# Where the moving operands of the dense products lie in SBUF: right end instead of beside the weights, xs tiles 2112 bytes apart

## The chip, the cores and the metric

One NeuronCore of one Trainium2 chip runs the whole program in one launch. The metric is device time in microseconds. The kernel before was timed in three runs.

## What is computed

The reference is a two-layer encoder trunk on 256 tokens of width 2048, with 256 memory tokens, all in float32. Cut to what matters here:

```python
for i in range(2):
    h = rmsnorm(x, norm_w[i])
    kv = rmsnorm(mem, mem_norm_w[i]) @ w_kv_mem[i]           # 2048 x 4096
    if i == 0:   # h @ w_in (14336 columns), windowed means, group product, cross-attention, SiLU gate
        y = pooling_branch(h, ...)
    else:        # h @ w_in (16512 columns), gated delta rule in chunks of 64, cross-attention, gate
        y = deltanet_branch(h, ...)
    x = x + y @ w_out[i]                                     # 6144 x 2048
return rmsnorm(x, final_norm_w)
```

Nearly all arithmetic is in products of some 256 rows of activations with large weight matrices that are read once.

## The kernel before, in words

Activations stand transposed: features on the 128 partitions, the 256 tokens along the row. A dense product forms 128 output features at a time. A weight block of 128x128 is the stationary operand, a tile of 128x256 is the moving one, and the sum over the input features builds up in one PSUM tile `pd`.

To keep float32 precision at the speed of the one-pass float32r format, each factor is split into a high and a low part. Weights arrive by DMA in units of 128 x 1024 floats (512 KB) into `wr` (`fetch`, L204, four buffers). ScalarE casts a unit into `wh` (L218), and VectorE forms `wl` = `wr` - `wh` (L220), three buffers each (`stage`, L211). A unit holds eight blocks of 128x128, each 512 bytes of a partition's row. An activation tile has shape [128, 2, 256]: its first 1024 bytes are the high part, the next 1024 the low part. Each 128x128 block then takes three matmuls, for instance in `dense` (L237):

```python
mm(ps, wh[:, kk, :], xh, k == 0, False)
mm(ps, wh[:, kk, :], xl, False, False)
mm(ps, wl[:, kk, :], xh, False, k == n - 1)
```

There are three kinds of these activation tiles. `xs` (16 buffers, written in `split_x`, L307) is the normalized input of a layer, the moving operand of the input product. The same buffers hold the raw memory tokens in `mem_tiles`, and in the last group the gated output (`new_y`, L414, with `last`). `y` (12 buffers) is the gated output, the moving operand of `out_piece` (L417). `ms` (16 buffers) holds the normalized memory tokens and later the pooled groups: the moving operand of the product for the keys in `mem_kv` (L373) and of the group product in `mix_jobs` (L607), and the stationary operand of the product for the values, in which `wh` and `wl` move with 512 columns. Other temporaries of the first part (softmax, decay gates) take turns in the `ms` buffers.

Buffers come from pools. `keep` and `work` last for the whole kernel, and `work` holds `wr`, `wh`, `wl`, `xs`, `y` and small tiles. `mp` holds `ms` and the attention's keys and values, and is given up before the second part, the delta rule, whose pool `gp` then takes its place.

TensorE's order is set by hand: `Flow` (L83) interleaves the dense jobs with the dependent chains (softmax, decay, matrix inversion, delta rule) by a small model of time. Line 184 is the matmul in the helper `mm`, so all matmuls but transposes have that line, and the tiles tell them apart.

Of the kernel before, what the change touches and what calls it, by code (L numbers as in the profile page):

```python
# [24 lines left out]
XA_SCALE = 512 ** -0.5  # L25
DN_SCALE = 128 ** -0.5

# buffers per tag, and dense steps between two looks at the chains
W_RAW_BUFS = 4
W_SPLIT_BUFS = 3  # L30
PS_DENSE = 3
# [1 line left out]
CHAIN_BUFS = 6  # L33
SQ_BUFS = 3
SLICE = 2
# priorities of the weight staging and of the parts of a chain on ScalarE and VectorE
P_STAGE = 600
P_UA = 600
P_INV = 600
P_NORM = 600  # L40
# how long the tensor engine leaves a step of a chain to the other engines, in units of US ns
US = 1300.0
Y_CONV = 9.0
Y_INV = 14.2
# [36 lines left out]


class Flow:  # L83
    """Interleaves dense weight products with the dependent chains, in the order the tensor engine issues them."""

    def __init__(self):
        self.now, self.tasks, self.jobs, self.active = 0.0, [], [], None
# [50 lines left out]
def trunk_kernel(  # L138
# [21 lines left out]

    keep = ctx.enter_context(tc.tile_pool(name="keep", bufs=1))
    work = ctx.enter_context(tc.tile_pool(name="work", bufs=2))
    psd = ctx.enter_context(tc.tile_pool(name="psd", bufs=PS_DENSE, space=PSUM))
    psa = ctx.enter_context(tc.tile_pool(name="psa", bufs=PS_CHAIN, space=PSUM))
    psk = ctx.enter_context(tc.tile_pool(name="psk", bufs=2, space=PSUM))

    def wt(shape, dt, tag, bufs):
        return work.tile(shape, dt, tag=tag, name=tag, bufs=bufs)

    def pa(n):  # L170
        t = psa.tile([P, 512], F32, tag="a", name="pa")
# [135 lines left out]
    def split_x(layer, row):  # L307
        for k in range(KT):
            xn = wt([P, S], F32, "xn", SQ_BUFS)
            V.scalar_tensor_tensor(  # L310
                out=xn, in0=xT[:, k, :], scalar=small[:, SM_NW + layer * KT + k : SM_NW + layer * KT + k + 1],
                in1=row, op0=ALU.mult, op1=ALU.mult,
            )
            xs[k] = wt([P, 2, S], F32R, "xs", KT)
            split_to(xs[k], xn)
            yield 0.7

# [3 lines left out]
    def mem_tiles(layer):  # L321
        if layer == 0:
            tiles = []
            for c in range(8):
                fetch(c + 1 if c < W_RAW_BUFS else W_RAW_BUFS)
                mt = wt([P, 2, S], F32, "xs", KT)
                nc.sync.dma_start(out=mt, in_=mem_d[:, 2 * c : 2 * c + 2, :])
                tiles.append(mt)
            for c in range(8):
                if c < W_SPLIT_BUFS:  # L330
                    stage(c + 1)
                mem_split(layer, 2 * c, tiles[c])
            return tiles
        for c in range(8):
            mt = wt([P, 2, S], F32, "xs", KT)
            nc.gpsimd.dma_start(out=mt, in_=mem_d[:, 2 * c : 2 * c + 2, :])
            mem_split(layer, 2 * c, mt)
            yield 0.8
# [3 lines left out]
    def mem_split(layer, k0, mt):  # L342
        for i in range(2):
            k = k0 + i
            w = small[:, SM_MW + layer * KT + k : SM_MW + layer * KT + k + 1]
            t = mp.tile([P, 2, S], F32R, tag="ms", name="ms", bufs=KT)
            A.activation(out=t[:, 0, :], in_=mt[:, i, :], func=AF.Copy, scale=w)  # L347
            V.scalar_tensor_tensor(  # L348
                out=t[:, 1, :], in0=mt[:, i, :], scalar=w, in1=t[:, 0, :].bitcast(F32),
                op0=ALU.mult, op1=ALU.subtract,  # L350
            )
            ms[k] = t
# [59 lines left out]
        return g  # L412

    def new_y(last=False):  # L414
        return wt([P, 2, S], F32R, "xs", KT) if last else wt([P, 2, S], F32R, "y", 12)

    def out_piece(src, ys, nk, *flags, acc=None, done=None):  # L417
        per = HC // nk
# [38 lines left out]
    def softmax_chain(layer, h, q, pT, done):  # L457
        yield 0.6
        kT = kv["k", layer]
        sc = pa(512).rearrange("p (s m) -> p s m", s=2)  # L460
        for st in range(2):
            for kk in range(4):
                mm(sc[:, st, :], q[kk][:, st * P : (st + 1) * P], kT[:, 4 * h + kk, :], kk == 0, kk == 3)
        mx = wt([P, 2], F32, "mx", 2)
        V.tensor_reduce(out=mx, in_=sc, axis=AX.X, op=ALU.max)
        nb = wt([P, 2], F32, "nb", 2)
        V.tensor_scalar(out=nb, in0=mx, scalar1=-XA_SCALE, scalar2=None, op0=ALU.mult)
        p = mp.tile([P, 2, S], F32, tag="ms", name="xp", bufs=KT)
        sm = wt([P, 2], F32, "smx", 2)
        for st in range(2):  # L470
            A.activation(
                out=p[:, st, :], in_=sc[:, st, :], func=AF.Exp, bias=nb[:, st : st + 1], scale=XA_SCALE,
                accum_out=sm[:, st : st + 1],
            )
        rs = wt([P, 2], F32, "rs", 2)
        V.reciprocal(out=rs, in_=sm)
        V.tensor_scalar(out=rs, in0=rs, scalar1=0.5, scalar2=None, op0=ALU.mult)
        for st in range(2):
            V.tensor_scalar(
                out=p[:, st, :], in0=p[:, st, :], scalar1=rs[:, st : st + 1], scalar2=None, op0=ALU.mult  # L480
            )
        yield 5.0
        pt = pa(512).rearrange("p (m s) -> p m s", m=2)
        for mt in range(2):
            for st in range(2):
                transpose(pt[:, mt, st * P : (st + 1) * P], p[:, st, mt * P : (mt + 1) * P], ident)
        t = mp.tile([P, 2, S], F32, tag="ms", name="xpt", bufs=KT)
        for mt in range(2):
            A.activation(out=t[:, mt, :], in_=pt[:, mt, :], func=AF.Copy, scale=rmem["col"][:, mt : mt + 1])
        pT[h] = t  # L490
        done.set(flow.now + 1500)

    def attention(layer, wsrc, ct_q, ct_g, xready, kvready):
# [5 lines left out]
        def q_jobs(h):  # L499
            q = [None] * 4  # L500

            def mk(kk):
                def post(ps):
                    if kk % 2 == 0:
                        q2 = mp.tile([P, 2, S], F32, tag="ms", name="xq", bufs=KT)
                        q[kk], q[kk + 1] = q2[:, 0, :], q2[:, 1, :]
                    A.copy(out=q[kk], in_=ps)
                    if kk == 3:
                        flow.spawn(softmax_chain(layer, h, q, pT, soft[h]))

                return post

            for kk in range(4):
                dense([wsrc[ct_q + 4 * h + kk, i] for i in range(2)], get_xs, mk(kk), xready, kvready)
# [19 lines left out]

    mp_cm = tc.tile_pool(name="mp", bufs=1)
    mp = mp_cm.__enter__()
    mem_ready, mem_done, x_ready, kv_ready = Flag(), Flag(), Flag(), Flag()

    def start_up():
# [33 lines left out]
    def u_jobs(g):  # L573
        for c in range(8):
            def post(ps, c=c):
                if c == 0:
                    cnts[g] = mp.tile([P, S], F32, tag="ms", name="cnt", bufs=KT)
                    nc.gpsimd.dma_start(out=cnts[g], in_=cnt_d[:, g, :])
                    if g == 0:
                        V.tensor_scalar(  # L580
                            out=scale_h, in0=small[:, SM_PS : SM_PS + 32], scalar1=0.5, scalar2=None, op0=ALU.mult
                        )
                u = ub[c % 2]
                A.copy(out=u[:, 8 : S + 8], in_=ps)
                src, n = u, S + 16
                for lv in range(g + 1):
                    step = 1 << lv
                    n -= step
                    dst = mp.tile([P, S + 16], F32, tag="ms", name="pacc", bufs=KT)
                    V.tensor_tensor(out=dst[:, 0:n], in0=src[:, 0:n], in1=src[:, step : step + n], op=ALU.add)  # L590
                    src = dst
                off = 8 - WINDOWS[g] // 2
                m = wt([P, S], F32, "xn", SQ_BUFS)
                V.tensor_tensor(out=m, in0=src[:, off : off + S], in1=cnts[g], op=ALU.mult)
                V.tensor_tensor(out=m, in0=m, in1=u[:, 8 : S + 8], op=ALU.subtract)
                t = mp.tile([P, 2, S], F32R, tag="ms", name="ms", bufs=KT)
                split_to(t, m)
                pooled[g][c] = t
                if c == 7:
                    pflag[g].set(flow.now + 5000)  # L600
# [91 lines left out]
        flow.spawn(decay_chain(ps))  # L692

    def decay_chain(ps):
        mask = mp.tile([P, 2, P], F32, tag="ms", name="mask", bufs=KT)
        nc.gpsimd.dma_start(out=mask, in_=cst_d[:, CS_MASK:CS_W].rearrange("p (d m) -> p d m", d=2))
        V.tensor_copy(out=identr, in_=ident)
        V.tensor_copy(out=selr, in_=cst[:, CS_SEL : CS_SEL + 64])
# [7 lines left out]
        V.tensor_scalar(out=nwh, in0=small[:, SM_DN : SM_DN + 1], scalar1=0.5, scalar2=None, op0=ALU.mult)  # L706

        def mt(shape, name):
            return mp.tile(shape, F32, tag="ms", name=name, bufs=KT)

        cum = [[mt([P, 384], "cum") for _ in range(2)] for _ in range(2)]
        for d in range(2):
# [58 lines left out]
    g_jobs(3)  # L771
    n_first = len(flow.jobs)

    # second part: the jobs of the delta-rule groups
    kqs = [[None] * 4 for _ in range(8)]
    kq_state = [None] * 8
    kq_done = [Flag() for _ in range(8)]
# [445 lines left out]
    engines = ENGINES  # L1223
    with tc.manual_schedule(engines=engines):
        flow.run(len(flow.jobs) - n_first)
    mp_cm.__exit__(None, None, None)
    gp = ctx.enter_context(tc.tile_pool(name="gp", bufs=1))
    gpool.append(gp)
# [159 lines left out]
```

## Time and profile before

| | |
|---|---|
| median of three runs | 2592.03 us |
| lowest and highest run | 2589.52 and 2594.63 us |
| span of the profiled execution | 2590.5 us |
| mean granted clock of TensorE | 0.998 |
| instructions in the profile | 53005 |

The profile is one execution with a span of 2590.5 us from the first to the last instruction. No time of its own is listed for that execution beside the span; the span lies between the lowest and the highest of the three runs, and 1.5 us below their median. A matmul's duration in the profile reaches from its start to the modelled end of its pipeline, so durations of successive matmuls overlap, and the busy share says little on the rate; the distance from one start to the next gives the rate.

### The profile page before, as it was taken

The numbers are of one execution on the slowest core, as the hardware profiler recorded it, in microseconds if no ns is written. First come the engines' busy times: TensorE is split into PE (matmuls) and PEld (weight loads), VectorE is DVE, ScalarE is ACT, GpSimd is POOL, SyncE is SP. The second block draws the span as 40 slices with busy tenths as digits, with TensorE's granted clock in tenths as the row PEclk, the third lists the DMA queues.
The fourth block names the chain that finished last, engine by engine and source line by source line (L and its number), as shares of the span: only waits on it lengthen the run. The fifth ranks groups of instructions, "written<-read, shape, count | busy, mean of one in ns | idle before, by whom it ended". The sixth has DMA issues, their size and how long they took to land.

```text
span 2590.5 us, 53005 instructions
## 1 busy us (share of the span) xinstructions
PE 2566.3 (99%) x21996; PEld 2510.7 (97%) x21996; DVE 1788.2 (69%) x3317; ACT 1238.0 (48%) x1946; POOL 15.5 (1%) x44
## 2 busy tenths in 40 slices
PE   8999999999999999999999999999999999999998
PEld 7899999999999999998999999999999999999998
DVE  6564455656557576674546557989889797979786
ACT  5444434434444443554344445555545555565544
POOL 0000000000000000000000000000000000000000
PEclk9999999999999999999999999999999999999999
DMA  7654455555555555655554545535344454535353
GB/s 241 219 185 160 159 172 166 184 185 187 184 185 187 184 185 187 204 190 189 190 186 156 164 161 167 167 116 164 127 155 136 138 163 133 164 127 166 125 175 103
DMA packets 120817, 436.17 MB, mean 168 GB/s; under 512 B 13728, under 2 KB 13984, under 8 KB 120576
## 3 DMA queue, kind: packets, MB, share of 16 engines
q1 hardware_dynamic: 118080, 426.06, 50.4%
q0 software_dynamic: 1776, 5.64, 0.7%
q8 instruction: 172, 2.82, 0.4%
q10 hardware_dynamic: 720, 1.08, 0.1%
q14 instruction: 69, 0.57, 0.1%
HBM read 430.63 MB, written 2.10 MB: 167 GB/s over the span
## 4 chain that ended last, share of the span: by engine, by line
PE 96%; DVE 2%; ACT 1%; issue 0%; DMA 0%; POOL 0%; DVEq 0%
PE pd L184 86%; PE pa L184 9%; PE kk L184 1%; DVE wl L220 1%; PE pa L188 0%; ACT wh L218 0%; DMA xs<-in_mem_dram 0%; DVE ms L348 0%; DVE o L1264 0%; DMA wr<-in_wv_dram 0%; DVE Dg L983 0%; DVE cacc L795 0%; DVE L L985 0%; ACT ms L347 0%; DVE itmp L993 0%
## 5 line engine op out<-in xcount | busy, mean ns | idle before, releaser
L220 DVE TENSOR_TENSOR wl<-wr,wh 128x1024 fp32r<-128x1024 f32 x802 | 981.1, 1223 | 609.1 <-ACT wh L218 607.2
L184 PE MATMUL pd<-xs,wh 128*128 128x256 f32 x7328 | 1351.4, 286 | 2.8 <-DVE gt L411 2.1
L218 ACT CAST wh<-wr 128x1024 fp32r<-128x1024 f32 x802 | 841.0, 1049 | 1043.3 <-PE pd L184 839.8
L184 PEld LDWEIGHTS pd<-xs,wh 128*128 128x128 f32 x7328 | 1143.5, 192 | 7.4 <-DVE gt L411 2.3
L184 PE MATMUL pd<-xs,wl 128*128 128x256 f32 x3664 | 1036.5, 283 | 0.0
L184 PEld LDWEIGHTS pd<-xs,wl 128*128 128x128 f32 x3664 | 702.1, 192 | 0.0
L184 PE MATMUL pd<-y,wh 128*128 128x256 f32 x2944 | 524.0, 280 | 1.1 <-DVE y L258 1.1
L184 PEld LDWEIGHTS pd<-y,wh 128*128 128x128 f32 x2944 | 449.7, 187 | 1.8 <-DVE y L258 1.3
L184 PE MATMUL pd<-y,wl 128*128 128x256 f32 x1472 | 410.7, 279 | 0.0
L184 PEld LDWEIGHTS pd<-y,wl 128*128 128x128 f32 x1472 | 276.6, 188 | 0.0
L184 PE MATMUL pd<-ms,wh 128*128 128x256 f32 x1536 | 271.4, 279 | 0.0
L184 PEld LDWEIGHTS pd<-ms,wh 128*128 128x128 f32 x1536 | 234.8, 188 | 0.2
L184 PE MATMUL pd<-ms,wl 128*128 128x256 f32 x768 | 214.9, 280 | 0.0
L184 PE MATMUL pd<-wh,ms 128*128 128x512 f32 x512 | 163.4, 398 | 6.2 <-ACT ms L347 6.2
L184 PEld LDWEIGHTS pd<-ms,wl 128*128 128x128 f32 x768 | 144.3, 188 | 0.0
L795 DVE SCALAR_TENSOR_TENSOR cacc<-cu,small,cacc 128x256 f32<-128x256 f32 x256 | 122.5, 482 | 5.7 <-ACT cacc L793 1.3
L184 PEld LDWEIGHTS pd<-wh,ms 128*128 128x128 f32 x512 | 96.7, 189 | 29.2 <-ACT ms L347 6.2
L447 DVE TENSOR_TENSOR xT<-xT,pd 128x512 f32<-128x512 f32 x140 | 95.8, 684 | 41.2 <-PE pd L184 41.0
L184 PE MATMUL pd<-wl,ms 128*128 128x512 f32 x256 | 102.0, 398 | 0.3 <-DVE wl L220 0.2
L993 DVE TENSOR_TENSOR itmp<-L,Ti 128x126 f32<-128x126 f32 (+22 forms) x248 | 62.6, 252 | 2.3
L999 DVE TENSOR_TENSOR Ti<-Ti,itmp 128x126 f32<-128x126 f32 (+22 forms) x248 | 62.7, 253 | 2.2
L257 ACT CAST y<-yf 128x256 fp32r<-128x256 f32 x92 | 35.9, 405 | 55.7 <-DVE yf L525 54.0
(217 smaller groups left out, 1778.5 us busy)
## 6 DMA issues: line engine op xcount, KB each, us to landing
wr<-in_dw_dram SPq DMA_DIRECT2D x258, 512.0 KB, 3.5
wr<-in_pw_dram SPq DMA_DIRECT2D x192, 512.0 KB, 3.5
wr<-in_wo_dram SPq DMA_DIRECT2D x192, 512.0 KB, 3.5
wr<-in_wv_dram SPq DMA_DIRECT2D x64, 512.0 KB, 3.6
wr<-in_wk_dram SPq DMA_DIRECT2D x64, 512.0 KB, 3.5
wr<-in_pg_dram SPq DMA_DIRECT2D x32, 512.0 KB, 3.5
xs<-in_mem_dram SPq DMA_DIRECT2D x8, 256.0 KB, 7.1
xT<-in_x_dram SPq DMA_DIRECT2D x4, 512.0 KB, 6.3
```

The source lines that it names most:

```text
L184: T.matmul(out, lhsT=lhsT, rhs=rhs, start=start, stop=stop)
L218: A.copy(out=hi, in_=raw)
L220: V.tensor_tensor(out=lo, in0=raw, in1=hi.bitcast(F32), op=ALU.subtract)
L257: A.copy(out=dst[:, 0, :], in_=src)
L447: V.tensor_tensor(out=xv, in0=xv, in1=pss[0], op=ALU.add)
L795: V.scalar_tensor_tensor(out=a, in0=u[:, k : k + S], scalar=cwh[:, ct, k : k + 1], in1=a, op0=ALU.mult, op1=ALU.add)
L993: V.tensor_tensor(out=tv, in0=L[:, j + 1 : 32, j : j + 1].to_broadcast([P, n, c]), in1=Ti[:, j : j + 1, 0:c].to_broadcast([P, n, c]), op=A ...
L999: V.tensor_tensor(out=Ti[:, j + 1 : 32, 0:c], in0=Ti[:, j + 1 : 32, 0:c], in1=tv, op=ALU.subtract)
```

## The change

Two pools are added that take their space from the right end of SBUF. `act` holds `xs` and `y`, for the whole kernel. `mr` holds everything with the tag `ms` and is given up together with `mp`. An `xs` tile gets 16 more floats at its end that nobody uses, so that two neighbours start 2112 bytes apart instead of 2048. The rest of the diff replaces comments by empty lines.

```diff
+X_PAD = 16
...
     work = ctx.enter_context(tc.tile_pool(name="work", bufs=2))
+    act = ctx.enter_context(tc.tile_pool(name="act", bufs=1, side="right"))
...
+    def xt(dt):
+        t = act.tile([P, 2 * S + X_PAD], dt, tag="xs", name="xs", bufs=KT)
+        return t[:, 0 : 2 * S].rearrange("p (a s) -> p a s", a=2)
...
-            xs[k] = wt([P, 2, S], F32R, "xs", KT)
+            xs[k] = xt(F32R)
...
-                mt = wt([P, 2, S], F32, "xs", KT)
+                mt = xt(F32)
...
-            t = mp.tile([P, 2, S], F32R, tag="ms", name="ms", bufs=KT)
+            t = mr.tile([P, 2, S], F32R, tag="ms", name="ms", bufs=KT)
...
-        return wt([P, 2, S], F32R, "xs", KT) if last else wt([P, 2, S], F32R, "y", 12)
+        return xt(F32R) if last else act.tile([P, 2, S], F32R, tag="y", name="y", bufs=12)
...
     mp = mp_cm.__enter__()
+    mr_cm = tc.tile_pool(name="mr", bufs=1, side="right")
+    mr = mr_cm.__enter__()
...
+    mr_cm.__exit__(None, None, None)
     mp_cm.__exit__(None, None, None)
```

The other lines of the diff turn `mp.tile(..., tag="ms", ...)` into `mr.tile(...)` and `wt(..., "xs", KT)` into `xt(...)` in the same way.

The built program has the same instructions on every engine before and after, in the same order and with the same semaphore waits; only addresses differ. In bytes of a partition's row:

| tiles | before: first tile, distance | after: first tile, distance |
|---|---|---|
| `wr` x4 | 40096, 4096 | 40096, 4096 |
| `xs` x16 | 56480, 2048 | 170976, 2112 |
| `wh` x3 | 89248, 4096 | 56480, 4096 |
| `wl` x3 | 101536, 4096 | 68768, 4096 |
| `y` x12 | 132064, 2048 | 204768, 2048 |
| `ms` x16 | 161472, 2048 | 138208, 2048 |

Weight blocks lie 512 bytes apart, and the two halves of an activation tile 1024, so for a pair of tiles the difference of the two addresses, taken modulo 512, is the same for all blocks and halves. This table gives that remainder, moving tile less weight tile:

| product | before | after |
|---|---|---|
| `xs` with `wh` or `wl` (10992 matmuls) | 0 | 0, 64, 128, 192, 256, 320, 384, 448: 1350 to 1398 matmuls each |
| `y` with `wh` or `wl` (4416 matmuls) | 320 | 320 |
| `ms` with `wh` or `wl` (2304 matmuls) | 32 | 320 |
| `wh` or `wl` moving, `ms` stationary (768 matmuls) | 480 | 192 |

## Rows read from the trace of the kernel before

**Rows 1.** Page, busy time: engine, us, share of the span, instructions; TensorE's clock in slices.
```profile
span 2590.5 us, 53005 instructions
PE 2566.3 (99%) x21996; PEld 2510.7 (97%) x21996; DVE 1788.2 (69%) x3317; ACT 1238.0 (48%) x1946; POOL 15.5 (1%) x44
...
PEclk9999999999999999999999999999999999999999
```

**Rows 2.** Page, the chain that ended last: shares of the span by engine, by line.
```profile
PE 96%; DVE 2%; ACT 1%; issue 0%; DMA 0%; POOL 0%; DVEq 0%
PE pd L184 86%; PE pa L184 9%; PE kk L184 1%; DVE wl L220 1%; PE pa L188 0%; ACT wh L218 0%; DMA xs<-in_mem_dram 0%; DVE ms L348 0%; DVE o L1264 0%; DMA wr<-in_wv_dram 0%; DVE Dg L983 0%; DVE cacc L795 0%; DVE L L985 0%; ACT ms L347 0%; DVE itmp L993 0%
```

**Rows 3.** Waits of TensorE, longest first: us in total, times, longest us.
```profile
PE pd L184 <- ACT ms L347: 6.2, 1, 6.2
PE pa L188 <- DVE itmp L993: 2.2, 1, 2.2
...
PE pd L184 <- DVE wl L220: 0.2, 1, 0.2
```

**Rows 4.** TensorE's groups by line and tiles: shape, count, busy us, mean ns, idle before.
```profile
L184 PE MATMUL pd<-xs,wh 128*128 128x256 f32 x7328 | 1351.4, 286 | 2.8 <-DVE gt L411 2.1 <-ACT xs L257 0.6
L184 PE MATMUL pd<-xs,wl 128*128 128x256 f32 x3664 | 1036.5, 283 | 0.0
L184 PE MATMUL pd<-y,wh 128*128 128x256 f32 x2944 | 524.0, 280 | 1.1 <-DVE y L258 1.1
L184 PE MATMUL pd<-y,wl 128*128 128x256 f32 x1472 | 410.7, 279 | 0.0
L184 PE MATMUL pd<-ms,wh 128*128 128x256 f32 x1536 | 271.4, 279 | 0.0
L184 PE MATMUL pd<-ms,wl 128*128 128x256 f32 x768 | 214.9, 280 | 0.0
L184 PE MATMUL pd<-wh,ms 128*128 128x512 f32 x512 | 163.4, 398 | 6.2 <-ACT ms L347 6.2
L184 PE MATMUL pd<-wl,ms 128*128 128x512 f32 x256 | 102.0, 398 | 0.3 <-DVE wl L220 0.2
```

**Rows 5.** Windows, tile pd alone: stretch, length, each engine's busy us (count), PEclk, DMA, GB/s.
```profile
454.00:494.00 40.00, 40.00 (x336) 40.00 (x335) 0.00 (x0) 2.57 (x7) 1.00 0.58 188
655.00:695.00 40.00, 40.00 (x342) 40.00 (x342) 4.82 (x7) 0.36 (x1) 1.00 0.58 185
1260.00:1290.00 30.00, 30.00 (x259) 30.00 (x258) 2.12 (x5) 0.00 (x0) 1.00 0.57 192
...
1150.00:1210.00 60.00, 60.00 (x259) 48.29 (x258) 0.00 (x0) 3.50 (x6) 1.00 0.57 186
```

**Rows 6.** Timeline of TensorE, last output piece: start us, us from first start to last end.
```profile
2560.02 0.28 PE L184 MATMUL pd<-xs,wl 128*128 128x256 f32 x1
2560.14 0.40 PE L184 MATMUL pd<-xs,wh 128*128 128x256 f32 x2
2560.38 0.28 PE L184 MATMUL pd<-xs,wl 128*128 128x256 f32 x1
```

**Rows 7.** Timeline of TensorE at 1700 us, where a chain's matmuls hand over to xs.
```profile
1700.47 0.48 PE L184 MATMUL pd<-xs,wh 128*128 128x256 f32 x2
1700.79 0.28 PE L184 MATMUL pd<-xs,wl 128*128 128x256 f32 x1
1700.91 0.40 PE L184 MATMUL pd<-xs,wh 128*128 128x256 f32 x2
1701.14 0.28 PE L184 MATMUL pd<-xs,wl 128*128 128x256 f32 x1
```

**Rows 8.** Page, the two steps of weight staging: count, busy us, mean ns.
```profile
L220 DVE TENSOR_TENSOR wl<-wr,wh 128x1024 fp32r<-128x1024 f32 x802 | 981.1, 1223 | 609.1 <-ACT wh L218 607.2
...
L218 ACT CAST wh<-wr 128x1024 fp32r<-128x1024 f32 x802 | 841.0, 1049 | 1043.3 <-PE pd L184 839.8
```

**Rows 9.** Window of the second part, all engines: PE, PEld, DVE, ACT, POOL.
```profile
1900.00:2100.00 200.00, 200.00 (x2036) 197.70 (x2036) 168.97 (x416) 114.02 (x217) 1.07 (x2) 1.00 0.44 141
```

More of the change, by code (lines that the diff above doesn't have):

```diff
@@ L334, in mem_tiles @@
         for c in range(8):
-            mt = wt([P, 2, S], F32, "xs", KT)
+            mt = xt(F32)
             nc.gpsimd.dma_start(out=mt, in_=mem_d[:, 2 * c : 2 * c + 2, :])
@@ L467, in softmax_chain @@
         V.tensor_scalar(out=nb, in0=mx, scalar1=-XA_SCALE, scalar2=None, op0=ALU.mult)
-        p = mp.tile([P, 2, S], F32, tag="ms", name="xp", bufs=KT)
+        p = mr.tile([P, 2, S], F32, tag="ms", name="xp", bufs=KT)
         sm = wt([P, 2], F32, "smx", 2)
@@ L486, in softmax_chain @@
                 transpose(pt[:, mt, st * P : (st + 1) * P], p[:, st, mt * P : (mt + 1) * P], ident)
-        t = mp.tile([P, 2, S], F32, tag="ms", name="xpt", bufs=KT)
+        t = mr.tile([P, 2, S], F32, tag="ms", name="xpt", bufs=KT)
         for mt in range(2):
@@ L504, in post @@
                     if kk % 2 == 0:
-                        q2 = mp.tile([P, 2, S], F32, tag="ms", name="xq", bufs=KT)
+                        q2 = mr.tile([P, 2, S], F32, tag="ms", name="xq", bufs=KT)
                         q[kk], q[kk + 1] = q2[:, 0, :], q2[:, 1, :]
@@ L576, in post @@
                 if c == 0:
-                    cnts[g] = mp.tile([P, S], F32, tag="ms", name="cnt", bufs=KT)
+                    cnts[g] = mr.tile([P, S], F32, tag="ms", name="cnt", bufs=KT)
                     nc.gpsimd.dma_start(out=cnts[g], in_=cnt_d[:, g, :])
@@ L588, in post @@
                     n -= step
-                    dst = mp.tile([P, S + 16], F32, tag="ms", name="pacc", bufs=KT)
+                    dst = mr.tile([P, S + 16], F32, tag="ms", name="pacc", bufs=KT)
                     V.tensor_tensor(out=dst[:, 0:n], in0=src[:, 0:n], in1=src[:, step : step + n], op=ALU.add)
@@ L595, in post @@
                 V.tensor_tensor(out=m, in0=m, in1=u[:, 8 : S + 8], op=ALU.subtract)
-                t = mp.tile([P, 2, S], F32R, tag="ms", name="ms", bufs=KT)
+                t = mr.tile([P, 2, S], F32R, tag="ms", name="ms", bufs=KT)
                 split_to(t, m)
@@ L694, in decay_chain @@
     def decay_chain(ps):
-        mask = mp.tile([P, 2, P], F32, tag="ms", name="mask", bufs=KT)
+        mask = mr.tile([P, 2, P], F32, tag="ms", name="mask", bufs=KT)
         nc.gpsimd.dma_start(out=mask, in_=cst_d[:, CS_MASK:CS_W].rearrange("p (d m) -> p d m", d=2))
@@ L708, in mt @@
         def mt(shape, name):
-            return mp.tile(shape, F32, tag="ms", name=name, bufs=KT)
+            return mr.tile(shape, F32, tag="ms", name=name, bufs=KT)
         cum = [[mt([P, 384], "cum") for _ in range(2)] for _ in range(2)]
```

## The prediction

> **What bounds the kernel now.** I read the page first, then TensorE's waits, its groups, and stretches that hold one kind of product alone. TensorE is busy for 99% of the span, at a granted clock near 1.00 in every slice, which is the 2.4 GHz level [rows 1]. The chain that ended last is TensorE for 96%, and matmuls into `pd`, the dense products, for 86% [rows 2]. All that TensorE waits for in sight are single waits of 6.2 and 2.2 us and shorter ones; weight staging holds it up once, for 0.2 us [rows 3]. So the time is the number of matmuls times the distance from one start to the next, and the question is what sets that distance.
>
> The groups say who they are: 7328 + 3664 = 10992 matmuls with `xs` moving, 2944 + 1472 = 4416 with `y`, 1536 + 768 = 2304 with `ms`, all of 256 columns, and 512 + 256 = 768 of 512 columns in which the weights move [rows 4]. The durations there overlap and are no rate, but they already differ: 283 and more with `xs`, 279 and 280 with `y` and `ms`, for the same shape [rows 4].
>
> The rate comes from windows that hold one kind only. In each, the count includes the matmuls that began earlier and reach in: with one lasting 0.283 us and starts 0.12 us apart, about 2.4. `xs`: 40 us / (336 - 2.4) = 119.9 ns. `y`: 40 / (342 - 2.4) = 117.8 ns. `ms`: 30 / (259 - 2.4) = 116.9 ns. Weights moving with 512 columns (0.398 us long, 1.7 too many): 60 / (259 - 1.7) = 233.2 ns [rows 4, 5]. At 2.4 GHz, 256 columns are 106.7 ns, so each kind pays something on top: 13.2 ns with `xs`, 11.1 with `y`, 10.2 with `ms`.
>
> Is that the address or the code? The last output piece answers it. It runs the code of the other output pieces, with the same number of blocks per output, but its moving tiles lie in `xs` buffers: three matmuls from 2560.02 to 2560.38 us, 120 ns each [rows 6], as in the input product and not as in the `y` pieces. The clock is the same, and DMA busy shares are alike in the pure `xs`, `y` and `ms` windows (0.57 and 0.58) [rows 5]. **So where the moving tile lies costs 2.1 ns of 120**, and the change alters just that.
>
> A second observation says how. After a chain's matmuls the first `xs` matmul is followed 0.20 us later by the next (0.48 less 0.28), and then starts stand 0.12 apart or a little under: from 1700.79 to 1701.14, three matmuls take 0.35 us, 117 ns each [rows 7]. The same addresses run at the quicker rate for a few matmuls and at 120 once the stream is long. That looks like two regular streams that fall into step, the moving tile and the next weights, which `xs` alone meets at remainder 0 (modulo 512) in every matmul. This is my reading; no row shows two reads colliding.
>
> **The change part by part.** No instruction is added, removed or moved, and no wait or queue changes, so there is no fixed cost to count. What can change is the distance between starts, kind by kind.
>
> 1. `xs`, 10992 matmuls. After the change the remainder is 320 plus a multiple of 64, another one for each tile, so a block's three matmuls meet one remainder and the next three another. Only two of sixteen tiles have remainder 0, and three matmuls are too few to fall into the slow step. The nearest row for a remainder that isn't 0 is `y` with 320: 117.8 ns. Saving: 10992 x (119.9 - 117.8) = 23 us. Bounds: nothing, if the tiles stay at 119.9; at best the rate of `ms`, 10992 x (119.9 - 116.9) = 33 us; a loss is not excluded by any row, because six of the eight remainders have never been seen (see the rivals).
>
> 2. `y`, 4416 matmuls. The remainder against the weights stays 320, the weights themselves move by exactly 32768 bytes. I take 0. Bounds: 4416 x 0.9 = 4 us gained at the rate of `ms`, 4416 x 2.1 = 9 us lost at that of `xs`.
>
> 3. `ms`, 2304 matmuls. The remainder goes from 32 to 320, that of `y`. I take the rate of `y`: 2304 x (117.8 - 116.9) = 2 us lost. Bounds: 0, and 2304 x 3.0 = 7 us lost.
>
> 4. Weights moving, 768 matmuls of 512 columns: remainder from 480 to 192, and no row has 192. If they lose as `ms` does, in proportion to the columns, 768 x 1.8 = 1.4 us; I take 2 us lost. Bounds: 0 and 768 x 6 = 5 us.
>
> 5. Other instructions at new addresses (VectorE and ScalarE on `xs`, `y`, `ms`, the pool `gp`): I cost them at 0. What hides them is TensorE, busy throughout [rows 1]; if an operation grew, VectorE has room: 169 us of 200 in a full stretch of the second part [rows 9].
>
> 6. What is late next, when TensorE is quicker? A weight unit serves 24 matmuls, 2.88 us before and 2.83 after. Staging one takes 1.05 us of ScalarE and 1.22 us of VectorE [rows 8], so it keeps pace. Chain waits were covered by dense matmuls, and the cover shrinks by about 2%; the waits that show now are 2.2 us and less after the start [rows 3], so I allow 1 us, inside the rounding.
>
> Sum: 23 - 2 - 2 = 19 us less. Against the profiled span that is 2590.5 - 19 = 2571.5 us. The span stands 1.5 us under the median of the runs, which I add back: 2573 us.
>
> The Trainium skill speaks against this change. "SBUF — State Buffer", section "Who interferes with whom", gives TensorE two independent read ports, one for the moving operand and one for the weights, and says that it never waits on another engine. By that rule placement would be inert, and the sum 0. The trace does not agree as far as `xs` and `y` go: 119.9 against 117.8 ns, in the same code.
>
> **The rivals.**
>
> *Only the last seven bits count.* Remainders modulo 128 separate the three kinds as well (0, 64, 32). Then half of the new `xs` tiles are as before, and the saving is halved: 11 - 4 = 7 us, 2585 us with the offset. For it: nothing in the trace separates 128 from 512. Against it: the tiles alternate, so the slow step hardly has time to set in.
>
> *Distance, not remainder.* By address the order is `xs` slowest, then `y`, then `ms`, which is also their distance from the weights. If that were the cause, `xs` and `y` at the far end would reach the rate of `ms`: 33 + 4 = 37 us less, 2555 us. Against it: the quick start after a chain at the same addresses [rows 7].
>
> *Placement doesn't matter once the stream is long,* or the whole difference comes from something else about the `xs` buffers that moves along with them. Then `xs` stays at 119.9, `ms` perhaps loses 2 to 4 us: 2592 to 2596 us. Against it: the last output piece [rows 6]. The skill's rule on the ports, above, would give this outcome too.
>
> *Slower: untried remainders are worse.* Six of the eight, or 8244 matmuls, stand at remainders that no row shows. If each cost as much above `xs` as `xs` costs above `ms`, 3.0 ns, that is 25 us lost, the two known ones give back 3, `ms` and the 512-column products lose 4: 2592 + 26 = 2618 us. It decides from the point where the mean of `xs` passes 119.5 ns, since 4 us of loss elsewhere are 0.4 ns on each of 10992 matmuls. For it: new offsets at each block might keep the two streams from ever settling. Against it: unsettled stretches are the quicker ones [rows 7].
>
> **How the numbers follow.** Forecast 0.46 (2566 to 2580 us), seven bits 0.16, distance 0.18, no effect 0.12, worse remainders 0.08. A range from 2554 to 2590 us leaves out the last two, 0.20. A change of 0.2% is 5.2 us, about what a measurement of this kernel can tell from none. Faster than 2586.8 us: the first three, but for 0.02 of the seven-bit case, 0.78. Within 0.2%: no effect and those 0.02, less 0.01 that goes to slower, 0.13. Slower: 0.09.
>
> **What the profile after would show.** If right: the window quotient for `xs` near 117.8 ns and its durations near 279 in the groups, `y` unchanged at 117.8, `ms` a little up, towards 117.8; the last output piece no longer at 120.0. Distance would show as `y` falling to 117; seven bits as `xs` near 119. I am wrong if `xs` stays at 119.9 or goes above it, or if the matmuls gain and waits of TensorE of more than a few us appear in the second part.

## The result, and the profile after

| | before | after |
|---|---|---|
| median | 2591.06 us (4 runs) | 2576.39 us (4 runs) |
| lowest and highest run | 2589.52, 2594.63 us | 2574.03, 2577.42 us |
| span of the profiled execution | 2590.5 us | 2573.9 us |

The ratio of the times is 0.994 with a 95% interval from 0.9926 to 0.9954: the change makes the kernel faster by 0.6%. The spans differ by 16.6 us.

The page of the kernel after, busy time, clock, and the chain that ended last:

```profile
span 2573.9 us, 53005 instructions
PE 2549.3 (99%) x21996; PEld 2493.6 (97%) x21996; DVE 1787.5 (69%) x3317; ACT 1237.2 (48%) x1946; POOL 15.5 (1%) x44
...
PEclk9999999999999999999999999999999999999999
...
PE 97%; DVE 2%; ACT 1%; DMA 0%; issue 0%; POOL 0%; DVEq 0%
```

The instructions are as many as before, the clock is the same, and TensorE's busy time fell by 17.0 us, about as much as the span [rows 1, 2]. VectorE and ScalarE are within 1 us of before. TensorE's longest waits after:

```profile
PE pd L191 <- ACT ms L354: 6.0, 1, 6.0
PE pa L195 <- DVE itmp L1002: 2.3, 1, 2.3
PE pd L191 <- DVE gt L418: 2.2, 1, 2.2
```

Against [rows 3] and the wait for `gt` in [rows 4] each is within 0.2 us, so no new wait took the place of the time gained. What changed stands in TensorE's groups (line and tiles, shape, count, busy us, mean ns, idle before); the matmul of `mm` is now line 191:

```profile
L191 PE MATMUL pd<-xs,wh 128*128 128x256 f32 x7328 | 1332.6, 283 | 2.9 <-DVE gt L418 2.2 <-ACT xs L264 0.6
L191 PE MATMUL pd<-xs,wl 128*128 128x256 f32 x3664 | 1028.0, 281 | 0.0
L191 PE MATMUL pd<-y,wh 128*128 128x256 f32 x2944 | 523.9, 280 | 1.1 <-DVE y L265 1.1
...
L191 PE MATMUL pd<-ms,wh 128*128 128x256 f32 x1536 | 273.0, 280 | 0.0
...
L191 PE MATMUL pd<-wh,ms 128*128 128x512 f32 x512 | 163.5, 399 | 6.0 <-ACT ms L354 6.0
```

The two `xs` groups lost 18.8 and 8.5 us of busy time (durations overlap, so this is no sum), `y` with `wh` kept its own to 0.1 us, `ms` with `wh` grew by 1.6 us [rows 4]. The same four windows as in [rows 5], tile `pd` alone, and a fifth in the last output piece:

```profile
454.00:494.00 40.00, 40.00 (x341) 40.00 (x340) 0.00 (x0) 2.54 (x7) 1.00 0.58 191
655.00:695.00 40.00, 40.00 (x342) 40.00 (x342) 4.82 (x7) 0.00 (x0) 1.00 0.58 190
1260.00:1290.00 30.00, 30.00 (x257) 30.00 (x256) 2.12 (x5) 0.00 (x0) 1.00 0.55 180
1150.00:1210.00 60.00, 60.00 (x258) 48.34 (x258) 0.00 (x0) 3.50 (x6) 1.00 0.58 189
...
2544.00:2560.00 16.00, 16.00 (x137) 16.00 (x136) 4.10 (x6) 0.00 (x0) 1.00 0.11 36
```

By the quotient that the prediction used, `xs` went from 119.9 to 40 / (341 - 2.4) = 118.1 ns, `y` stayed at 117.8, `ms` went from 116.9 to 30 / (257 - 2.4) = 117.8. The 512-column products are one count off, which is within what a window resolves. The last output piece, 120.0 ns a matmul before [rows 6], is at 16 / (137 - 2.4) = 118.9.

A finer gauge is the distance between two rows of TensorE's timeline where the moving tile changes. From the first `xs` row of a group of eight blocks to the first `y` row of an output piece lie 384 matmuls, and again 384 from there to the next `xs` row. Before (start us, us from first start to last end):

```profile
608.15 0.40 PE L184 MATMUL pd<-xs,wh 128*128 128x256 f32 x2
...
654.23 0.40 PE L184 MATMUL pd<-y,wh 128*128 128x256 f32 x2
...
699.46 0.41 PE L184 MATMUL pd<-xs,wh 128*128 128x256 f32 x2
```

and after:

```profile
604.85 0.41 PE L191 MATMUL pd<-xs,wh 128*128 128x256 f32 x2
...
650.23 0.40 PE L191 MATMUL pd<-y,wh 128*128 128x256 f32 x2
...
695.46 0.41 PE L191 MATMUL pd<-xs,wh 128*128 128x256 f32 x2
```

Before, `xs` takes 46.08 us / 384 = 120.0 ns and `y` 45.23 / 384 = 117.8; after, 45.38 / 384 = 118.2 and 45.23 / 384 = 117.8. All experiments below are read at these three rows; `xs`, `y` and `ms` rates are given in that order, `ms` from the 768 matmuls of the second layer's keys in the same way (116.7 before, 117.8 after).

Over the whole trace, the mean distance between the starts of dense matmuls that nothing holds up is, in ns: `xs` 119.80 before and 118.16 after, `y` 117.79 and 117.78, `ms` 117.12 and 117.83, 512 columns 233.3 and 233.3. Times the counts that is 10992 x 1.64 = 18.0 us gained and 2304 x 0.71 = 1.6 us lost: 16.4 us of the 16.6.

### The profile page after: what moved, and what is told of

It is laid out like the page before. It is cut to its first block, busy times and chain, and to the rows that moved or that the text cites. A ratio compares the mean times of both kernels' runs of the same rounds, so it can differ in the third digit from the quotient of the medians.

```text
span 2573.9 us, 53005 instructions
## 1 busy us (share of the span) xinstructions
PE 2549.3 (99%) x21996; PEld 2493.6 (97%) x21996; DVE 1787.5 (69%) x3317; ACT 1237.2 (48%) x1946; POOL 15.5 (1%) x44
## 4 chain that ended last, share of the span: by engine, by line
PE 97%; DVE 2%; ACT 1%; DMA 0%; issue 0%; POOL 0%; DVEq 0%
PE pd L191 87%; PE pa L191 9%; PE kk L191 1%; PE pa L195 0%; DVE wl L227 0%; ACT wh L225 0%; DMA xs<-in_mem_dram 0%; DVE ms L355 0%; DVE o L1274 0%; DMA wr<-in_wv_dram 0%; ACT ms L354 0%; DVE L L994 0%; DVE cacc L804 0%; DVE Dg L992 0%; DVE yf L1143 0%
## 5 line engine op out<-in xcount | busy, mean ns | idle before, releaser
L191 PE MATMUL pd<-xs,wh 128*128 128x256 f32 x7328 | 1332.6, 283 | 2.9 <-DVE gt L418 2.2
L191 PEld LDWEIGHTS pd<-xs,wh 128*128 128x128 f32 x7328 | 1125.6, 189 | 7.5 <-DVE gt L418 2.4
L191 PEld LDWEIGHTS pd<-xs,wl 128*128 128x128 f32 x3664 | 690.1, 188 | 0.0
```

The costliest lines, as they stand in the source:

```text
L191: T.matmul(out, lhsT=lhsT, rhs=rhs, start=start, stop=stop)
```

## The experiments

Theory: the distance between starts depends on the remainder of the two addresses (moving tile less weights), and nothing else about the place counts. Rivals: the end of SBUF or the distance counts; the moving tile's own address counts; only seven bits of the remainder count. Below, "remainder" is modulo 512 unless said otherwise. All kernels but two start from the kernel after, with `xs` tiles 2048 bytes apart again, and shift the three kinds of tiles by unused tiles ahead of them, so that each kind has one remainder throughout. The dense matmuls come in the same order in all, and the only added instructions are one to three `memset`s of the unused tiles (`all_r320` and `pad_left` have none).

### Position alone, then the spare bytes alone

`all_r320` takes the spare bytes out of the change: all three kinds stand at 320.

```diff
-X_PAD = 16
+X_PAD = 0
+PADS = (0, 0, 0)
...
+    acty = right("acty", PADS[0])
+    act = right("actx", PADS[1])
```

`right` opens a pool at the right end, and ahead of it an unused tile of so many floats, none for 0; it is printed with the next kernels.

> The changed kernel with its spare 64 bytes per xs tile taken away (position alone): xs, y and ms all lie at remainder 320 to the weights. Remainder theory: xs runs at the rate that y has at 320, 117.8 ns, 0.4 ns under the changed kernel's 118.2, so 10992 x 0.4 = 4 us less than the changed kernel, a ratio near 0.9925 to before. Mixing theory (a different offset for each tile is what breaks the slow step): without it xs goes back towards 120 ns, some 20 us more than the changed kernel.

Measured: 2574.36 us, ratio to before 0.9931 (0.9916 to 0.9946). The kernel after has 0.994 (0.9926 to 0.9954), so the two can't be told apart: moving the tiles alone gives a gain of that size, and the 2112-byte distance adds none that shows. `xs` did not go back to 120 ns, so mixing the remainders isn't needed for the gain. The rates are better than after (means of 117.7 for `xs` and 117.1 for `y`, worth 8.5 us), but the gaps behind dense matmuls of 256 columns (distances of over 130 ns to the next start) hold 41 us above the regular distance, against 34 after, which takes 7 of that back; why they grew was not tried.

`pad_left` is the kernel before with the spare bytes alone; everything stays at the left end.

```diff
+    def xt(dt):
+        return wt([P, 2 * S + 16], dt, "xs", KT)[:, 0 : 2 * S].rearrange("p (a s) -> p a s", a=2)
...
-            xs[k] = wt([P, 2, S], F32R, "xs", KT)
+            xs[k] = xt(F32R)
```

> The kernel before with only the spare 64 bytes added to each xs tile, all pools where they were: xs meets the eight remainders, y stays at 320, ms at 32. Remainder theory: xs near 118.2 ns as in the changed kernel, ms at its 116.9, about 2574 us, ratio near 0.993. Distance theory: xs stays beside the weights and at 120 ns, ratio 1.000.

Measured: 2565.68 us, ratio 0.9901 (0.9885 to 0.9918). Half of the change, without the move, is faster than the whole of it. TensorE's timeline of `pad_left`:

```profile
602.66 0.40 PE L187 MATMUL pd<-xs,wh 128*128 128x256 f32 x2
...
648.02 0.39 PE L187 MATMUL pd<-y,wh 128*128 128x256 f32 x2
...
691.54 0.40 PE L187 MATMUL pd<-xs,wh 128*128 128x256 f32 x2
```

`xs` runs as after (45.36 / 384 = 118.1 ns), so mixing remainders is worth the same at either end. The surprise is `y`: 43.52 / 384 = **113.3 ns**, at the remainder 320 at which it has 117.8 before and after. Of the 4083 `y` matmuls in long streams (60 and more in a row), 2071 ran at 113.3 here, and none before or after; the mean of all `y` is 115.7. That is 4416 x 2.1 = 9.3 us, and `ms`, which stays at 32, doesn't lose its 1.6 us: 10.9 together, the 10.7 us by which it beats the change. So one remainder can have two steady rates, called steps below. This none of the theories had.

### All kinds at one remainder: 0 and 32

`all_r0` and `all_r32` put all three kinds at the right end at one remainder (spare floats ahead of `y`, `xs`, `ms`; for `all_r32` 72 instead of 80):

```diff
+PADS = (80, 0, 0)
...
+    def right(name, n=0):
+        if n:
+            spare = ctx.enter_context(tc.tile_pool(name=name + "s", bufs=1, side="right"))
+            nc.gpsimd.memset(spare.tile([P, n], F32, name=name + "s"), 0.0)
+        return ctx.enter_context(tc.tile_pool(name=name, bufs=1, side="right"))
```

> The changed kernel without the spare bytes, and with xs, y and ms shifted so that all three meet the weights at remainder 0, still at the right end. Remainder theory: all three kinds at 120.0 ns; against the kernel before y loses 4416 x 2.2 = 10 us and ms 2304 x 3 = 7 us, about 2608 us, ratio 1.006. Distance theory: as fast as the changed kernel, 0.994.

Measured: 2603.07 us, ratio 1.0044 (1.0029 to 1.0059).

```profile
610.70 0.40 PE L200 MATMUL pd<-xs,wh 128*128 128x256 f32 x2
...
656.77 0.40 PE L200 MATMUL pd<-y,wh 128*128 128x256 f32 x2
...
702.85 0.40 PE L200 MATMUL pd<-xs,wh 128*128 128x256 f32 x2
```

46.07 and 46.08 us for 384: 120.0 ns for both, and `ms` has 120.0 as well. At the right end, as far from the weights as in the change, remainder 0 gives the rate that `xs` had before. Distance and the end of SBUF are out. `y` loses 4416 x 2.17 = 9.6 us and `ms` 2304 x 2.87 = 6.6 by the means over the trace, and the 512-column products gain 768 x 6.4 = 4.9 (226.9 ns, not 233.3), which the expectation had left out: 11.3 us, and the span grew by 11.1.

> The same with all three at remainder 32, where ms was before. Remainder theory: xs and y go to the 116.7 to 116.9 ns that ms had there; against the kernel before xs gains 10992 x 3.0 = 33 us and y 4416 x 0.9 = 4 us, about 2554 us, ratio 0.986. If the rate of ms came from something else than its remainder (its region, or the order of its tiles): xs and y near 117.8 ns, ratio 0.9925.

Measured: 2559.43 us, ratio 0.9876 (0.9861 to 0.989); 116.7 ns for each of the three kinds at those rows, the rate that `ms` had before at 32. So a rate goes with the remainder from one kind of tile to another.

### The other remainders

Four kernels with three remainders each, one run apiece, differ from `all_r0` in one line, `PADS`: `sweep_a` (56, 8, 112), `sweep_b` (32, 8, 112), `sweep_c` (8, 8, 72), `sweep_d` (104, 8, 112).

> Position as in the changed kernel, no spare bytes; xs at remainder 64, y at 96, ms at 128 (weights moving: 384). Seven bits: xs as 320 (117.8 or, once in that step, 113.3 ns), y unknown, ms as 0 (120.0). Nine bits: each remainder has steps of its own, ms need not be at 120. Time between 2530 and 2600 us.

> xs at remainder 160, y at 192, ms at 224 (weights moving: 288). Seven bits: xs as 32 (116.7 ns), y as 320 (117.8 or 113.3), ms as 96 in the run before. Nine bits: none of these need hold. If xs is at 116.7, about 2560 us.

> xs at remainder 256, y at 288, ms at 480 (weights moving: 32). Seven bits: xs as 0, 120.0 ns, and y as 32, 116.7 ns: about 2590 us. Nine bits: xs off 120.

> xs at remainder 384, y at 416, ms at 448 (weights moving: 64). Seven bits: xs as 0, 120.0 ns; y as 32, 116.7; ms as 320, 117.8 or 113.3: about 2590 us. Nine bits: xs off 120.

Times: 2581.43, 2567.08, 2593.60 and 2573.51 us, beside 2592.06 for the kernel before. Seven bits failed here already: `xs` at 160 ran at 117.3, 118.7 and 120.0 ns and in no long stream at the 116.7 of 32, and `xs` at 384 mostly at 118.7, not at 120.0. A fifth, `sweep_e` (24, 96, 48), came later, to set 352 beside 224: they agree modulo 128 and differ modulo 256.

> Right end, xs at remainder 352, y at 224, ms at 160, each 256 bytes from one measured: eight bits say xs as y at 96, 120.0 ns; y as ms at 480, 118.3; ms as xs at 160 and y at 416, 117.3 or 118.6 or 120. About 2592 us. A rate elsewhere in any of the three would say that the ninth bit counts.

It took 2600.71 us, the slowest but one of all. The expected 2592 us had left out that `y` and `ms` lose at these remainders: 118.3 and 118.6 ns on average, some 6 of the 8.4 us by which the span grew. Its timeline:

```profile
610.60 0.40 PE L200 MATMUL pd<-xs,wh 128*128 128x256 f32 x2
...
656.67 0.40 PE L200 MATMUL pd<-y,wh 128*128 128x256 f32 x2
...
702.11 0.40 PE L200 MATMUL pd<-xs,wh 128*128 128x256 f32 x2
```

`xs` at 352: 46.07 / 384 = 120.0 ns. `y` at 224: 45.44 / 384 = 118.3. In one kernel, the same seven bits have two rates. All steady rates seen, ns a matmul of 256 columns (in `sweep_a` to `sweep_e`, `before`, `after` and the kernels of one remainder):

| remainder modulo 256 | remainders modulo 512 that were run | steady rates |
|---|---|---|
| 0 | 0, 256 | 120.0 |
| 32 | 32, 288 | 116.7, 117.8 |
| 64 | 64, 320 | 117.8, 113.3 |
| 96 | 96, 352 | 120.0 |
| 128 | 128, 384 | 118.7, 120.0 |
| 160 | 160, 416 | 117.3, 118.7, 120.0 |
| 192 | 192, 448 | 113.3, 117.8 |
| 224 | 224, 480 | 118.3 |

The rows with one rate are the plain ones: 0 and 256 are alike, 96 and 352, 224 and 480, while 96 and 224 differ. So seven bits of the difference are too few, and nothing here needs a ninth (113.3 was seen at 320 and not at 64, but 64 was run in one kernel only). Where a row has several rates, they come from different stretches. Only multiples of 32 bytes were tried.

### The best remainders, on either side

In `sweep_b`, 2632 of the 4083 `y` matmuls in long streams, at 192, had 113.4 ns, and in `sweep_d`, `ms` at 448 had 113.4. So all three kinds were put at 448 (`PADS = (96, 0, 0)`) and at 192 (`PADS = (32, 0, 0)`).

> xs, y and ms all at remainder 448, where every long ms stream of the sweep ran at 113.3 ns. If the remainder alone sets the step: all three kinds at 113.3, xs gains 10992 x 6.5 = 71 us on before, y 4416 x 4.5 = 20, ms 2304 x 3.8 = 9: about 2490 us, ratio 0.961. If each remainder has several steps and the way in decides (as y at 320 and 192 had 113.3 and 117.8): a mixture of both, 2500 to 2550 us. If it depends on the tiles' places beyond the remainder: nothing below 117 for xs, 2565 us or more.

> The same at remainder 192, 256 bytes from 448. Eight bits (remainders 256 apart act alike): the same rates as at 448 within the mixture of 113.3 and 117.8 ns, 2490 to 2550 us. Nine bits: it may differ, with fewer streams at 113.3, as y had in the sweep at 192 (2632 of 4083 long-stream matmuls at 113.4).

Measured: `all_r448` 2528.59 us, ratio 0.9761 (0.974 to 0.9782); `all_r192` 2533.27 us, ratio 0.9766 (0.9751 to 0.9781). The timeline of `all_r448`:

```profile
589.59 0.39 PE L200 MATMUL pd<-xs,wh 128*128 128x256 f32 x2
...
633.11 0.39 PE L200 MATMUL pd<-y,wh 128*128 128x256 f32 x2
...
676.63 0.39 PE L200 MATMUL pd<-xs,wh 128*128 128x256 f32 x2
```

43.52 us for each 384: 113.3 ns for `xs` and for `y`. But not everywhere. Two windows of `all_r448`, tile `pd` alone, both `xs` at remainder 448 in the first layer's input product:

```profile
186.00:208.00 22.00, 22.00 (x197) 22.00 (x195) 0.42 (x1) 1.09 (x3) 1.00 0.60 192
264.00:286.00 22.00, 22.00 (x189) 22.00 (x189) 0.41 (x1) 1.10 (x3) 1.00 0.55 185
```

22 / (197 - 2.4) = 113.1 ns in the first, 22 / (189 - 2.4) = 117.9 in the second, at the same clock. Of 4513 `xs` matmuls in long streams, 3334 ran at 113.3 or 113.4 and the other 1179 at 117.8, and each of the 28 streams kept to one step throughout. Mean rates: `xs` 114.8, `y` 113.8, `ms` 113.4, 512 columns 229.2. Against before that would be 10992 x 5.0 + 4416 x 4.0 + 2304 x 3.7 + 768 x 4.2 = 84 us; the span fell by 68.2. About 12 us of the rest went into gaps: behind 309 dense matmuls of 256 columns the next start came over 130 ns later, with 46 us above the regular distance, against 274 and 34 us before. What is left, some 4 us, isn't assigned. TensorE's waits in `all_r448` tell where a part of it stands:

```profile
PE pd L200 <- DVE gt L427: 3.5, 2, 2.8
PE pa L204 <- DVE itmp L1014: 2.6, 1, 2.6
PE pa L200 <- DVE Pq L1056: 1.9, 4, 0.7
```

The wait for `gt` is 3.5 us in place of 2.1 [rows 4], and a wait for a chain's `Pq`, which TensorE doesn't have in `before`, now takes 1.9 us.

`left_r448` puts the same remainder into the kernel before, at the left end. `xs` keep the addresses that they had; the weights move by 64 bytes. `spare` allocates an unused tile of so many floats, once.

```diff
+                spare("sp1", 16)
                 hi = wt(shape, F32R, "wh", W_SPLIT_BUFS)
...
+        spare("sp2", 32)
         return wt([P, 2, S], F32R, "xs", KT) if last else wt([P, 2, S], F32R, "y", 12)
...
     mp = mp_cm.__enter__()
+    nc.gpsimd.memset(mp.tile([P, 72], F32, name="sp3"), 0.0)
```

> The kernel before with three spare tiles (64, 128 and 288 bytes) and nothing else: xs stays at its very address beside the weights, wh and wl move 64 bytes on, y and ms a few hundred, and all three meet the weights at remainder 448. If the remainder to the weights decides: as all_r448 at the right end, xs a mixture of 113.3 and 117.8 ns, 2520 to 2545 us, ratio near 0.977. If the moving tile's own address decides (all runs so far had the weights at the same offset): xs stays at 120.0 ns, and 2565 us or more. If the distance or the right end has a part: slower than all_r448 by 10 us or more.

Measured: 2528.04 us, ratio 0.9746 (0.9727 to 0.9765).

```profile
589.11 0.39 PE L190 MATMUL pd<-xs,wh 128*128 128x256 f32 x2
...
632.63 0.39 PE L190 MATMUL pd<-y,wh 128*128 128x256 f32 x2
...
676.15 0.39 PE L190 MATMUL pd<-xs,wh 128*128 128x256 f32 x2
```

113.3 ns again. An `xs` tile at its old address, 120.0 ns before in this stretch, takes 113.3 because the weights lie 64 bytes further on. So neither the tile's own address nor the end of SBUF decides, but the difference; this one displacement of the weights was tried. This kernel and `all_r448` beat the change by 48 us (1.9%) without its two right-hand pools being needed: some 480 unused bytes in a row of SBUF do it.

The four runs of `all_r448` were 2523.20, 2524.03, 2533.15 and 2533.50 us, those of `left_r448` 2522.77, 2523.55, 2532.53 and 2534.80. The profile of `all_r448` was taken at 2524.03, that of `left_r448` at 2534.80: in the first 3334 `xs` and 3506 `y` matmuls of the long streams ran at the quick step, in the second 2865 and 2376. The 1599 that differ, times 4.5 ns, are 7 us of the 10.7 us between the two spans. One stretch stands out: from 797 us on 2205 matmuls of `xs`, `y` and `ms` follow each other without a gap. After the first few, all of them ran at one step, 113.3 ns in `all_r448` and 117.8 in `left_r448`, as a window of each shows, tile `pd` alone (the first row `all_r448`, the second `left_r448`):

```profile
800.00:1040.00 240.00, 240.00 (x2121) 240.00 (x2119) 22.60 (x43) 8.50 (x23) 1.00 0.62 196
...
800.00:1040.00 240.00, 240.00 (x2040) 240.00 (x2039) 21.71 (x41) 8.23 (x22) 1.00 0.59 188
```

240 / (2121 - 2.4) = 113.3 ns and 240 / (2040 - 2.4) = 117.8. Over 2205 matmuls that is 9.9 us, about what separates the runs near 2523 us from those near 2533. The profile of `all_r192`, taken at 2532.94 us, has the slow step there too (2040 in the same window). In all three the stretch begins behind a weight load that waits for VectorE's `wl`; the rows stand in the same order of kernels:

```profile
796.89 0.19 PEld L200 LDWEIGHTS pd<-y,wl 128*128 128x128 f32 x1 [0.17 <-DVE wl L236]
...
796.38 0.19 PEld L190 LDWEIGHTS pd<-y,wl 128*128 128x128 f32 x1 [0.17 <-DVE wl L227]
```

`before`, `after` and the kernels at 0, 32 and 320 have no gap there: in these three the quicker matmuls come for a `wl` before it is ready. So runs seem to differ by which step such stretches take, though with three executions of three kernels that is a fit, not a proof.

## Why the prediction was right, step by step

The time came out at 2576.4 us, 3.4 us above the forecast and in its own range. The gain was 16.6 us of span where 19 were forecast: `xs` gave 5.0 us less than its term, and the two losses were 2.4 us smaller than theirs, so the misses cancel in part. Measured against the prediction's steps:

- **The rate depends on where the moving tile lies:** right, and shown by moving tiles with no instruction added but `memset`s of unused tiles. What counts is the remainder against the weights, modulo 256, where the prediction had 512. The Trainium skill's rule of two independent read ports, one for the moving operand and one for the weights ("SBUF — State Buffer", section "Who interferes with whom"), would have made this inert; steady rates of one instruction at one clock were 113.3 to 120.0 ns here, and the same matmuls took 2528 to 2603 us.
- **Term 1, `xs`:** the mis-sized term: 18.0 us instead of 23. The step that failed is "only two of sixteen tiles have remainder 0, and three matmuls are too few to fall into the slow step", with the rate of `y` for all. Sorted by remainder, `xs` after has means of 119.1 (0), 118.2 (64), 119.3 (128), 118.0 (192), 117.9 (256), 117.5 (320), 118.5 (384) and 116.7 (448), each distance counted for the matmul that it begins with; counted for the one that it ends with, the same sorting gives 117.6 to 118.6, so in a mixed stream a distance can't be put down to one remainder. Modulo 256, 0 and 256 are one case, so a quarter of the tiles meet what `xs` met before, and another quarter (128 and 384) meets a remainder whose steady rates are 118.7 and 120.0, not the 117.8 of `y`. The mixed stream is quicker than 120.0, but its mean stays at 118.2, above `y`, and its durations came to 283 and 281 ns, not near 279. That it came so close to the rate of `y` is in part luck: the steady rates of the six remainders that no row had shown range from 113.3 to 120.0.
- **Term 2, `y`:** 0 forecast, 117.79 to 117.78 measured. Right for this change; `pad_left` shows that it wasn't certain, since at the same remainder half of the `y` stream ran at 113.3 there.
- **Term 3, `ms`:** 2 us lost forecast, 1.6 measured, and at the rate of `y`, as taken.
- **Term 4, 512 columns:** 2 us lost forecast, 0 measured: 233.3 ns at 480 and at 192.
- **Terms 5 and 6:** terms 1 to 4 account for 16.4 of the 16.6 us, and no wait of TensorE grew by more than 0.5 us [rows 3]. Staging kept pace, as forecast; at the quick step of `all_r448` it doesn't everywhere.
- **"Unsettled stretches are the quicker ones":** seen at remainder 0, where the first six distances of an interrupted `xs` stream take 118.7 ns on average in `before` and the settled ones 120.0. At 448 it is the other way round: 116.6 ns at first in `all_r448`, and the settled stream is the quickest of all (113.3 ns). The kernel after, whose `xs` never settle, lies above the steady 116.7 of `all_r32`.

The rivals. *Only seven bits* fell with 160 and 384 in the sweep, and with 352 and 224 in `sweep_e`. *Distance* fell with `y` at 117.8 after the move and at 120.0 in `all_r0`. *No effect* fell with the result. *Untried remainders are worse* fell too: the mean of `xs` was 118.2 ns, under the 119.5 from which that rival decides, and no steady rate above 120.0 was seen at any of the sixteen remainders (multiples of 32). What the prediction missed was on the other side: remainders with a step of 113.3.

What stays open: that two reads of SBUF collide was argued, and no run here shows it directly. Nor is it known what decides which of two steps a stream takes at the same remainder. It falls where a stream begins anew, after chain matmuls or a late `wl`: within some eight matmuls it has settled, and it keeps the step until the next interruption, also where `xs`, `y` and `ms` take turns at one remainder. The same beginning, at 797 us, led to 113.3 ns in `all_r448` and to 117.8 in `left_r448` and `all_r192`; no experiment varied a beginning alone. Nor was it tried whether the alternation of three matmuls a block matters to the table.

## What to carry to other kernels

When TensorE is busy throughout, measure the distance between starts for each kind of moving tile separately; differences of 1 to 6% at the same shape and clock may come from addresses. Then vary the remainder (moving tile less weights, modulo 256) of one kind at a time by unused bytes ahead of it, without touching the instructions, and take the best for all kinds: here 192 (448 modulo 512) gave 63 us, the change 15. As one remainder can have two steps, several runs are needed before a placement is called better.

## What was not expected of the hardware

- One instruction stream, one clock, one remainder, and two steady rates: 113.3 and 117.8 ns at 64 and 192 (modulo 256), each kept for up to 2205 matmuls in a row.
- The order of quality differs by shape: products in which the weights move with 512 columns took 226.9 ns at remainder 0, where 256 columns took their longest, 120.0; they took 229 at 64 and 320 (`all_r448`, `all_r192`), and 233.3 at 480 and 192.
- The best steady rate, 113.3 ns, is still 6.6 ns above the 106.7 ns that the prediction works out for 256 columns at the 2.4 GHz level.
